# Softmax division, three PSUM reads and the loads of w_out moved between engines in a two-block network kernel

## The chip, the cores and the metric

The kernel runs on one core of a Trainium2 chip. The metric is the device time of one launch in microseconds: the median over runs, and beside it one profiled execution that gives the trace. All arithmetic is float32. The long projections run as three products of a high and a low part (written `hh`, `hl`, `wh`, `wl` below).

## The reference, cut to what matters

The program computes two blocks in series. The first (differential attention, pooling, a mixture of experts) is not touched by the change and takes the first 835 us of the trace. The second block has two layers, each on 512 tokens of width 1024. One layer is:

```
h    = rms_norm(x, norm_g[l]);  cols = split_columns(h @ w_in[l])
# gated delta rule ("Gdn"), chunks of 64 tokens, 6 heads, both directions
a_mat   = beta * (k k^T) * d_strict          # triangular system of a chunk
p_intra = (q k^T) * d_incl
u0, w   = triangular_solve(a_mat, [beta v, beta gam k])
scan over chunks: u = u0 - w s;  o = q_g s + p_intra u;  s = g_end s + k_d^T u
# latent attention ("mla"), 6 heads, blocks of 128 queries
p = softmax(q k^T);  y_mla = p v
# rwkv7 ("Rwkv"), a recurrence per token, evaluated in chunks with a triangular solve
# joined
mix = concat(y_gdn, y_mla, y_rwkv) * silu(cols.gate)
x   = x + mix @ w_out[l]
```

After two layers a last norm gives the output.

## The kernel before

**The stages of a layer.** In the trace, layer 0 of the second block is 835 to 1390 us and layer 1 is 1390 to 1930 us. A layer begins with `Project`: the columns of `h @ w_in`, 24 products of 128x128 by 128x512 for each column of 128 (`mm<-hh,wh`, `mm<-hl,wh`, `mm<-hh,wl`). Beside it runs `Gdn`. Its `take_v` transposes the v columns (`tr`) and copies both halves from PSUM into `VS`, one half by ScalarE (ACT), the other by VectorE (DVE). Its `keys` normalises `kt` on DVE and transposes it into `kq`. Its `squares` multiplies k by k (64x64 products into PSUM tile `x`, twelve for each of four token tiles) and multiplies the result into `M`. Its `decays` builds `DT` and multiplies it by the products of k and q, which DVE reads from PSUM. `inverse` solves the triangles on DVE, and `chain` goes through eight steps of the state.

When the projection is over, two streams share TensorE (PE). `Rwkv.prepare` builds the triangles of the third branch (`SC`, `RB`, `M`, and the products `mm<-XT,AO` and `mm<-LT,XT` of its solve). `mla` goes through 24 units of softmax: scores in PSUM, their maximum on DVE, the exponential with its sum on ACT, the reciprocal `rs` on DVE, `e*rs` on GpSimd (POOL, L2236), four transposes on PE, a copy on ACT, and the product `mo`. Then `Rwkv.states` (small products `kp`, `pu` and the state `ST`, eight steps) runs beside `Mix`, which multiplies the joined rows by w_out in groups of rows k = 0 to 2, 3 to 5 and 6 to 7.

**How w_out comes in.** `Mix.weights` loads one 128x1024 piece of w_out into a ring of two tiles `w`, ACT copies it rounded to the high part, and POOL subtracts to get the low part. `Mix.ahead` does the same early for k = 6 and 7 (for k = 7 the subtraction is left to DVE later). `Mix.rows` then makes, for each token tile, `tr<-mix`, `y` (DVE), `mh` (ACT), `ml` (POOL) and 18 products `mm<-w,mh`, `mm<-w,ml` of 128x512. In layer 0 the residual `xres` is also multiplied by `final_g` (tile `wf`) on DVE.

**What sets the order.** PE's order is written by hand-made streams: `Net.weave` runs the generator that is ready, and a generator yields the microseconds that it wants to wait. The clock of that game is `pe_us`, which `Net.matmul` and `Net.transpose` advance by a modelled price of each product. All other engines and the DMA queue of SyncE (SP) are ordered by a scheduler from data dependencies and priorities, and each engine then takes its instructions strictly in that order. So an instruction that waits holds all that stands behind it on its engine.

Of the kernel before, what the change touches and what calls it, by code (L numbers as in the profile page):

```python
# [1380 lines left out]
class Gdn:  # L1381
# [118 lines left out]
    def keys(self):  # L1500
# [11 lines left out]
        yield 14  # L1512
# [36 lines left out]
    def squares(self):  # L1549
# [3 lines left out]
        for t in range(NT):  # L1553
# [9 lines left out]
            for b in range(4):  # L1563
                q, o = quarter(b), 32 * (b % 2)
                nc.vector.tensor_tensor(M[q, :, us], KK[q, None, us, o:o + 32].to_broadcast([32, 2, 6, 32]), M[q, :, us], op=ALU.mult)  # L1565

# [180 lines left out]
class Rwkv:  # L1747
# [54 lines left out]
    def prepare(self, mud, xud):  # L1802
# [16 lines left out]
        with pool(tc, "rka", 1, "right") as tmp, pool(tc, "rks", 2, "right") as small, pool(tc, "rpa", 1, "right", PSUM) as psum:  # L1819
# [102 lines left out]
            def products(d):  # L1922
# [224 lines left out]
def mla(net, a, l, mchd, mixt, tabd):  # L2147

    tc, nc = net.tc, net.nc
    with ExitStack() as ctx:  # L2150
# [75 lines left out]
        def scores(n):  # L2226
# [9 lines left out]
            nc.gpsimd.tensor_scalar(e, e, rs, None, op0=ALU.mult)  # L2236
# [39 lines left out]

class Mix:


# [30 lines left out]
    def ahead(self):  # L2310

        w6 = self.p.tile([128, D], F32R, name="w6", tag="w6")
        self.weights(6, *self.wq[0], self.net.nc.gpsimd)
        self.weights(7, w6, None, None)
        self.wq = [self.wq[0], (w6, self.wq[1])]

    def load(self, k0, n, mix=None):

        net, nc = self.net, self.net.nc
        if k0 == 6:  # L2320
            self.wp = self.wq
            h, lo = self.wp[1]
            nc.vector.tensor_tensor(lo, self.w[:, 1], h.bitcast(F32), op=ALU.subtract)
        else:
            for j in range(n):
                self.weights(k0 + j, *self.wp[j], nc.gpsimd)
        if k0 == 0:
            for t in range(NT):
                nc.sync.dma_start(net.xres[:, t], self.xd[tok(t), :])
            if self.l == 0:  # L2330

                net.rsqrt(net.r1, net.r1)
                f = self.wf
                nc.sync.dma_start(f, dram(self.a["final_g"], 0, [[0, 128], [1, D]]))
                for t in range(NT):
                    nc.vector.scalar_tensor_tensor(net.xres[:, t], net.xres[:, t], net.r1[:, t:t + 1], f, op0=ALU.mult, op1=ALU.mult)
        nc.sync.dma_start(self.g[:, :n], self.gated[128 * k0:128 * (k0 + n), :].rearrange("(j p) s -> p j s", p=128))
# [56 lines left out]
def second(net, a, out, xstack, tabd, xd0, layers=2):  # L2394

    tc, nc = net.tc, net.nc
    with ExitStack() as ctx:
# [3 lines left out]
        for l in range(layers):  # L2401
# [132 lines left out]
```

## Time and profile before

| | |
|---|---|
| median of 3 runs | 1932.37 us (1925.56 to 1935.56) |
| profiled execution | 1931.57 us, span 1929.8 us |
| mean granted TensorE clock | 0.912 |
| PE busy | 1675.8 us, 87% of the span |
| DVE busy | 1062.8 us, 55% |
| ACT busy | 573.9 us, 30% |
| POOL busy | 548.8 us, 28% |

The span runs from the first to the last instruction, and the profiled execution's own time is 1.8 us longer. PE is the engine to follow: what is not PE work in the span is time in which PE waits, and a wait names the engine and line that ended it. The busy share of the other engines says little by itself, since they work in stretches.

### The profile page before, as it was taken

The page shows a single profiled execution, that of the slowest core. Times are in us where ns is not written, and L with a number is a line of the kernel's source. Part 1 is how long each engine was busy: PE and PEld are TensorE (multiplying, and loading weights), DVE is VectorE, ACT ScalarE, POOL GpSimd, SP SyncE. Part 2 cuts the span into 40 slices and gives each one's busy share as a digit, 9 for nine tenths or more (in the row PEclk, how much of TensorE's full clock was granted, in tenths as well). Part 3 has the DMA queues.
Part 4 walks back from the last instruction along what each step waited for, and adds up shares of the span by engine and source line. Part 5 has one row for each costly group of instructions (what it writes and reads, how often), then busy time and mean ns, then how long its engine had stood idle before and what let it go on. Part 6 is the DMA issues. An engine that isn't in the chain of part 4 may idle for free.

```text
span 1929.8 us, 34104 instructions
## 1 busy us (share of the span) xinstructions
PE 1675.8 (87%) x14010; PEld 1119.3 (58%) x14010; DVE 1062.8 (55%) x2260; ACT 573.9 (30%) x1134; POOL 548.8 (28%) x559
## 2 busy tenths in 40 slices
PE   5999998999999999968788978768896899888777
PEld 3986584454544444447576746545675677556455
DVE  2435534353434343357796476745867875667437
ACT  3345432212122121154322125331343231154312
POOL 1113111101010101045641154254354612544443
PEclk7899998999999999979898988888898899797888
DMA  9924626999999999532243120143422341301332
GB/s 308 243 94 151 245 66 250 392 393 394 407 402 397 395 406 398 211 112 77 55 148 73 57 75 2 43 138 99 120 74 70 106 110 63 80 1 28 106 118 80
DMA packets 243218, 337.10 MB, mean 175 GB/s; under 512 B 92768, under 2 KB 166160, under 8 KB 226224
## 3 DMA queue, kind: packets, MB, share of 16 engines
q1 hardware_dynamic: 241152, 329.88, 49.6%
q10 hardware_dynamic: 1152, 3.22, 0.5%
q8 instruction: 112, 1.84, 0.4%
q0 software_dynamic: 752, 1.76, 0.3%
q14 instruction: 50, 0.41, 0.1%
HBM read 310.84 MB, written 23.99 MB: 174 GB/s over the span
## 4 chain that ended last, share of the span: by engine, by line
PE 26%; DVE 16%; issue 5%; DMA 4%; POOL 3%; ACT 2%; SPq 0%; DVEq 0%; POOLq 0%; ACTq 0%
PE mm L149 18%; DVE au L1344 2%; PE mm L159 2%; DVE stmp L1342 2%; PE x L149 2%; PE tr L149 1%; PE pu L149 1%; PE kp L149 1%; DVE M L1565 1%; POOL w L2308 1%; DMA w<-in_w_out_dram 1%; DVE wl L1214 1%; PE tr L159 1%; DVE y L1289 1%; PE mo L149 1%
## 5 line engine op out<-in xcount | busy, mean ns | idle before, releaser
L149 PE MATMUL gu<-w,XT 128*64 128x512 f32 x1024 | 225.8, 594 | 0.0
L149 PE MATMUL mm<-hh,wh 128*128 128x512 f32 (+1 forms) x464 | 202.1, 436 | 1.9 <-DVE rw L1319 1.9
L149 PE MATMUL mm<-hl,wh 128*128 128x512 f32 (+1 forms) x464 | 187.3, 404 | 0.0
L149 PE MATMUL mm<-hh,wl 128*128 128x512 f32 (+1 forms) x464 | 187.2, 403 | 0.0
L928 POOL TENSOR_TENSOR yl<-y,yh 128x512 fp32r<-128x512 f32 x30 | 38.1, 1271 | 451.3 <-ACT yh L927 451.3
L149 PEld LDWEIGHTS gu<-w,XT 128*64 128x64 f32 x1024 | 72.1, 137 | 142.7 <-issue 135.6
L938 DVE TENSOR_TENSOR xres<-mm,xres 128x512 f32<-128x512 f32 x128 | 79.2, 681 | 90.6 <-PE mm L149 90.6
L1212 ACT ACTIVATE wh<-w 128x1024 fp32r<-128x1024 f32 (+1 forms) x54 | 57.0, 1055 | 192.8 <-PE mm L149 134.1
L149 PE MATMUL mm<-w,hT 128*64 128x512 f32 x512 | 113.4, 595 | 0.7 <-ACT hT L912 0.7
L149 PEld LDWEIGHTS mm<-hh,wh 128*128 128x128 f32 (+1 forms) x464 | 91.3, 197 | 27.9 <-issue 5.7
L149 PEld LDWEIGHTS mm<-hh,wl 128*128 128x128 f32 (+1 forms) x464 | 90.6, 195 | 21.0
L2236 POOL TENSOR_SCALAR e<-e,rs 128x512 f32<-128x512 f32 x48 | 79.1, 1651 | 80.0 <-DVE rs L2235 58.1
L149 PEld LDWEIGHTS mm<-hl,wh 128*128 128x128 f32 (+1 forms) x464 | 91.6, 197 | 17.5 <-DVE hl L1160 0.2
L1214 POOL TENSOR_TENSOR wl<-w,wh 128x1024 fp32r<-128x1024 f32 (+1 forms) x28 | 68.1, 2431 | 112.3 <-ACT wh L1212 101.7
L149 PE MATMUL mm<-wh,hh 128*128 128x256 f32 x320 | 94.0, 294 | 2.2 <-ACT hh L357 2.2
L149 PE MATMUL mm<-wh,hl 128*128 128x256 f32 x320 | 91.2, 285 | 4.2 <-DVE hl L359 4.0
L149 PE MATMUL mm<-w,mh 128*128 128x512 f32 x256 | 88.6, 429 | 6.7 <-ACT mh L2359 4.1
L149 PE MATMUL mm<-wl,hh 128*128 128x256 f32 x320 | 90.7, 284 | 1.6 <-DVE wl L381 1.6
L149 PEld LDWEIGHTS mm<-w,hT 128*64 128x64 f32 x512 | 35.3, 137 | 66.7 <-issue 61.7
L1342 DVE TENSOR_TENSOR stmp<-au 96x60 f32<-96x60 f32 (+29 forms) x120 | 60.2, 501 | 16.0 <-DMA au<-rmud 8.7
L872 ACT ACTIVATE X<-mm,ws 128x512 f32<-128x512 f32 x32 | 22.0, 689 | 151.9 <-DVE ws L869 128.7
L926 DVE SCALAR_TENSOR_TENSOR y<-mm,ws,g2b 128x512 f32<-128x512 f32 x32 | 24.0, 751 | 78.2 <-PE mm L149 78.2
(580 smaller groups left out, 3678.4 us busy)
## 6 DMA issues: line engine op xcount, KB each, us to landing
w<-in_w_gate_dram SPq DMA_DIRECT2D x64, 1024.0 KB, 13.0
w<-in_w_up_dram SPq DMA_DIRECT2D x64, 1024.0 KB, 13.0
w<-in_w_down_dram SPq DMA_DIRECT2D x64, 1024.0 KB, 9.8
w<-in_w_in_dram SPq DMA_DIRECT2D x52, 512.0 KB, 4.1
w<-in_w_ada_dram SPq DMA_DIRECT2D x24, 1024.0 KB, 8.4
w<-in_w_out_dram SPq DMA_DIRECT2D x16, 512.0 KB, 4.1
w<-in_w_in_dram SPq DMA_DIRECT2D x6, 1024.0 KB, 11.9
w<-in_w_out_dram SPq DMA_DIRECT2D x4, 1024.0 KB, 6.3
```

Source lines behind the costliest of these rows:

```text
L149: return self.nc.tensor.matmul(out, a, b, **kw)
L159: return self.nc.tensor.transpose(out, a, ident)
L872: nc.scalar.activation(X[:, 512 * i:512 * i + 512], ps, AF.Copy, scale=ws[:, 1:2])
L926: nc.vector.scalar_tensor_tensor(y, py, ws[:, 0:1], net.g2b[:, hs], op0=ALU.mult, op1=ALU.mult)
L928: (nc.vector if last else nc.gpsimd).tensor_tensor(yl[:, hs], y, yh[:, hs].bitcast(F32), op=ALU.subtract)
L938: nc.vector.tensor_tensor(net.xres[:, t, hs], po, net.xres[:, t, hs], op=ALU.add)
L1212: nc.scalar.activation(h[:, :, :m], w[:, :, :m], AF.Copy)
L1214: eng.tensor_tensor(lo[:, :, :m], w[:, :, :m], h[:, :, :m].bitcast(F32), op=ALU.subtract)
L1289: nc.vector.scalar_tensor_tensor(y[:, lo:hi], ps[:, lo + d:hi + d], cw[:, j, m:m + 1], y[:, lo:hi], op0=ALU.mult, op1=ALU.add)
L1342: nc.vector.tensor_tensor(tv, au[:n, :, j + 1:, j:j + 1].to_broadcast(sh), au[:n, :, j:j + 1, 0:j].to_broadcast(sh), op=ALU.mult)
L1344: nc.vector.tensor_tensor(au[:n, :, j + 1:, 0:j], au[:n, :, j + 1:, 0:j], tv, op=ALU.add)
L2236: nc.gpsimd.tensor_scalar(e, e, rs, None, op0=ALU.mult)
```

## The change

Eight edits, all in the second block but the first:

1. In the model of PE's order, a float32 product of at most 64x64x64 counts a third of what it did.
2. `take_v`: both halves are copied by ACT.
3. `keys` yields 19 in place of 14 before its transposes.
4. `squares`: the multiplications into `M` are done for two token tiles at once (16 in place of 32 over both layers, twice as wide).
5. `decays`: ACT copies k.q from PSUM into an SBUF tile, and one DVE multiplication does both directions (8 in place of 16).
6. `prepare`: the multiplications into `SC` and `RB` do both halves at once (16 in place of 32 of each).
7. `mla`: `e*rs` is an ACT activation with a scale in place of a POOL multiplication (48 of them).
8. w_out: a class `Raw` owns a ring of four tiles `w` and asks for the first four pieces as soon as `prepare` has been written; `Mix.load` asks for `mix` and `gate` first; the subtraction for the second piece of a group is on DVE; `xres` is raised in halves inside `rows`.

The core of the diff:

```diff
         if a.dtype == F32:
-            self.pe_us += 2 * max(n / 1200, m / 1200, 0.027)
+            us = 2 * max(n / 1200, m / 1200, 0.027)
+            self.pe_us += us / 3 if m <= 64 and n <= 64 and a.shape[0] <= 64 else us
...
-                (nc.vector.tensor_copy if h else nc.scalar.copy)(dst, pv[half(h)])
+                nc.scalar.copy(dst, pv[half(h)])
...
-        yield 14
+        yield 19
...
-            for b in range(4):
-                q, o = quarter(b), 32 * (b % 2)
-                nc.vector.tensor_tensor(M[q, :, us], KK[q, None, us, o:o + 32].to_broadcast([32, 2, 6, 32]), M[q, :, us], op=ALU.mult)
+            if t % 2:
+                us = slice(6 * t - 6, 6 * t + 6)
+                for b in range(4):
+                    q, o = quarter(b), 32 * (b % 2)
+                    nc.vector.tensor_tensor(M[q, :, us], KK[q, None, us, o:o + 32].to_broadcast([32, 2, 12, 32]), M[q, :, us], op=ALU.mult)
...
-            for d in range(2):
-                dv = DT[:, d, us].rearrange("p (a h) c -> p a h c", a=2)
-                nc.vector.tensor_tensor(dv, dv, ps[:, :, :192].rearrange("p a (h c) -> p a h c", h=3), op=ALU.mult)
+            kr = tmp.tile([128, 6, 64], F32, name="rh")
+            nc.scalar.activation(kr.rearrange("p (a h) c -> p a (h c)", a=2), ps[:, :, :192], AF.Copy)
+            nc.vector.tensor_tensor(DT[:, :, us], DT[:, :, us], kr[:, None].to_broadcast([128, 2, 6, 64]), op=ALU.mult)
...
-                    for par in range(2):
-                        nc.vector.tensor_tensor(SC[:, par], pv[:, par, :, 64:], mk[:, None, :].to_broadcast([128, 2, 128]), op=ALU.mult)
+                    nc.vector.tensor_tensor(SC, pv[:, :, :, 64:], mk[:, None, None, :].to_broadcast([128, 2, 2, 128]), op=ALU.mult)
...
-            nc.gpsimd.tensor_scalar(e, e, rs, None, op0=ALU.mult)
+            nc.scalar.activation(e, e, AF.Copy, scale=rs)
...
+class Raw(dict):
+    def __init__(self, net, ctx, a, l):
+        super().__init__()
+        self.net, self.a, self.l = net, a, l
+        self.pool = ctx.enter_context(pool(net.tc, "wo", 4, "right"))
+        for k in range(4):
+            self.load(k)
+    def load(self, k):
+        w = self[k] = self.pool.tile([128, D], F32, name="w")
+        self.net.nc.sync.dma_start(w, dram(self.a["w_out_2"], (self.l * D + 128 * k) * D, [[D, 128], [1, D]]))
...
-        w = self.w[:, k % 2]
-        nc.sync.dma_start(w, dram(self.a["w_out_2"], (self.l * D + 128 * k) * D, [[D, 128], [1, D]]))
+        nc, w = self.net.nc, self.raw.pop(k)
...
+        if k0 < 6:
             for j in range(n):
-                self.weights(k0 + j, *self.wp[j], nc.gpsimd)
+                self.weights(k0 + j, *self.wp[j], nc.vector if j == 1 else nc.gpsimd)
...
+        for k in range(k0 + 4, min(k0 + 7, KC)):
+            self.raw.load(k)
...
+                if fresh:
+                    nc.vector.scalar_tensor_tensor(xres[:, t, hs], xres[:, t, hs], net.r1[:, t:t + 1], self.wf[:, hs], op0=ALU.mult, op1=ALU.mult)
...
+                while raw is None:
+                    yield 0.5
...
             net.weave(prepare, others, until=prepare)
+            raw = Raw(net, third.ctx, a, l)
             net.weave(states, others, until=states)
```

Three places show what this does to the order of instructions (no times here, only the order in which each engine takes them).

SP's queue in layer 0 at the end of `mla`, where `mixt<-mo` writes a tile of attention output and `xres` is the residual, in the kernel before:

```order
388 L2329 DMA xres<-xd 128x1024 x2
389 L2258 DMA mixt_7547<-mo 384x1x128
390 L2329 DMA xres<-xd 128x1024 x2
391 L2305 DMA w<-in_w_out_dram 128x1024 x2
392 L2334 DMA wf<-in_final_g_dram 128x1024
393 L2337 DMA gate<-gated_7548 128x3x512
394 L2343 DMA mix<-mixd_7546 128x4x384
395 L2305 DMA w<-in_w_out_dram 128x1024 x3
```

The same place in the changed kernel:

```order
388 L2347 DMA xres<-xd 128x1024 x2
389 L2260 DMA mixt_7547<-mo 384x1x128
390 L2347 DMA xres<-xd 128x1024 x2
391 L2340 DMA mix<-mixd_7546 128x4x384
392 L2341 DMA gate<-gated_7548 128x3x512
393 L2350 DMA wf<-in_final_g_dram 128x1024
394 L2291 DMA w<-in_w_out_dram 128x1024 x8
395 L2354 DMA mix<-mixt_7547 128x1536
```

The first pieces of w_out stood behind the last `mixt` and two `xres`; now `mix`, `gate` and `wf` stand ahead of them as well, and all eight pieces stand in one block.

ACT in layer 0, from the last unit of `mla` to the first rows of `Mix`, where `w_...<-w` is the rounded copy of a piece of w_out and `mh<-y` the high part of a mixed row; the kernel before:

```order
541 L2306 ACTIVATE w_11873<-w 128x1024
542 L2306 ACTIVATE w_11874<-w 128x1024
543 L2306 ACTIVATE w_11875<-w 128x1024
544 L2359 ACTIVATE mh<-y 128x384 x5
545 L2306 ACTIVATE w_11873<-w 128x1024
```

The changed kernel:

```order
568 L2319 ACTIVATE w_11823<-w 128x1024
569 L2319 ACTIVATE w_11824<-w 128x1024
570 L2319 ACTIVATE w_11825<-w 128x1024
571 L2319 ACTIVATE w_11829<-w 128x1024
572 L2319 ACTIVATE w_12272<-w 128x1024
573 L2374 ACTIVATE mh<-y 128x384 x5
```

Two copies, those of pieces k = 6 (`w_11829`) and k = 7 (`w_12272`), have come in between the copies of k = 0 to 2 and the first `mh`. The tile of piece 6 is the one that held piece 2, and piece 7 is loaded into the tile that held piece 6, each after POOL's subtraction of the piece before.

PE in layer 0 at the end of `mla`, where `mm<-cst,e` are transposes of a softmax tile, in the kernel before:

```order
3063 L149 MATMUL mo<-t_11577,vt 64x128
3064 L149 MATMUL mm<-LT,XT 32x32 x64
3065 L149 MATMUL kp<-ST,KR 64x64 x8
3066 L159 MATMUL mm<-cst,e 128x128 x8
3067 L149 MATMUL pu<-rhs,LT 64x64 x8
3068 L149 MATMUL mo<-t_11593,vt 64x128
```

The changed kernel, from the last two `mo` of `mla` on:

```order
3079 L151 MATMUL mo<-t_11605,vt 64x128
3080 L151 MATMUL mo<-t_11620,vt 64x128
3081 L151 MATMUL mm<-XT,AO 32x32 x64
3082 L151 MATMUL mm<-LT,XT 32x32 x64
3083 L151 MATMUL kp<-ST,KR 64x64 x8
3084 L151 MATMUL pu<-rhs,LT 64x64 x8
```

`mm<-LT,XT`, with `mm<-XT,AO` ahead of it, and the first steps of `states` stood between the last units of `mla` and now follow after the last `mo`. In layer 1 all three places look alike, without `wf`.

## Rows read from the trace of the kernel before

**Rows 1.** Stretches of layer 0, busy by engine, clock, DMA share, GB/s.

```profile
core 0: us, PE busy (x) PEld busy (x) DVE busy (x) ACT busy (x) POOL busy (x), PEclk, DMA share, GB/s
870.00:1126.00 256.00, 217.46 (x2302) 171.52 (x2301) 179.03 (x300) 67.27 (x108) 100.99 (x114) 0.90 0.32 84
952.00:1009.00 57.00, 50.46 (x293) 39.72 (x292) 54.91 (x83) 12.94 (x18) 30.31 (x31) 0.94 0.34 103
1126.00:1272.00 146.00, 116.55 (x1228) 73.93 (x1228) 101.56 (x231) 62.41 (x139) 65.61 (x54) 0.86 0.13 32
1272.00:1311.00 39.00, 20.25 (x533) 15.78 (x529) 15.73 (x23) 8.23 (x13) 17.87 (x20) 0.67 0.53 174
```

**Rows 2.** Waits of PE, layer 0: waited for, us in total, times, longest.

```profile
PE tr L159 <- DVE VS L1444: 12.0, 3, 7.0
PE mm L149 <- DVE SC L1945: 10.8, 3, 5.8
...
PE mm L159 <- DVE sq L1874: 7.8, 3, 5.3
PE x L149 <- DVE DT L1601: 6.2, 1, 6.2
PE tr L159 <- DVE kt L1515: 5.0, 1, 5.0
...
PE mm L159 <- POOL e L2236: 3.0, 2, 1.6
```

**Rows 3.** Waits of PE, layer 1.

```profile
PE tr L159 <- DVE VS L1444: 11.4, 3, 6.3
PE tr L159 <- DMA mix<-mixd: 8.6, 1, 8.6
PE x L149 <- DVE DT L1601: 6.8, 1, 6.8
```

**Rows 4.** Groups by line, 870 to 1126: busy, mean ns, idle before.

```profile
L1444 DVE COPY VS<-tr 64x512 f32<-64x512 f32 x6 | 4.2, 695 | 5.4 <-ACT VS L1444 5.4
L1601 DVE TENSOR_TENSOR DT<-DT,x 128x384 f32<-128x384 f32 x8 | 4.0, 545 | 0.0
```

**Rows 5.** ACT's nearest operation to the new one, 870 to 1126.

```profile
L1292 ACT ACTIVATE th<-y 128x512 f32<-128x512 f32 x9 | 5.7, 629 | 7.6 <-DVE y L1289 7.6
```

**Rows 6.** Groups by line, 1126 to 1272, POOL and DVE.

```profile
L2236 POOL TENSOR_SCALAR e<-e,rs 128x512 f32<-128x512 f32 x22 | 36.4, 1657 | 41.5 <-DVE rs L2235 27.4 <-PE mm L149 10.6 <-DVE au L1344 2.4
L1874 DVE TENSOR_TENSOR s<-BB,cl 128x512 f32<-128x512 f32 x4 | 4.7, 1186 | 0.0
L1869 DVE TENSOR_TENSOR KR<-ci,rw 128x512 f32<-128x512 f32 x4 | 2.7, 680 | 0.0
```

**Rows 7.** PE in time around the start of Mix, layer 0.

```profile
1271.87 1.29 PE L149 MATMUL mm<-XT,AO 32*32 32x32 f32 x128
1286.38 1.09 PE L149 MATMUL mo<-t,vt 128*64 128x128 f32 x14 [0.38 <-ACT t L2244]
1303.57 0.90 PE L159 MATMUL tr<-cst,mix 128*128 128x128 f32 x3 [9.15 <-DMA mix<-mixd]
1311.00 0.80 PE L149 MATMUL mm<-w,ml 128*128 128x512 f32 x1 [1.73 <-POOL ml L2360]
```

**Rows 8.** ACT and POOL in time, the same place.

```profile
1296.26 1.06 ACT L2306 ACTIVATE w<-w 128x1024 fp32r<-128x1024 f32 x1 [9.93 <-DMA w<-in_w_out_dram]
1297.40 5.62 POOL L2308 TENSOR_TENSOR w<-w,w 128x1024 fp32r<-128x1024 f32 x2 [5.76 <-DMA w<-in_w_out_dram]
```

**Rows 9.** DMA issues of w_out: pieces, KB each, median us to landing.

```profile
w<-in_w_out_dram SPq DMA_DIRECT2D x16, 512.0 KB, 4.1
```

**Rows 10.** PE in time around the start of Mix, layer 1.

```profile
1806.96 1.61 PE L149 MATMUL mm<-XT,AO 32*32 32x32 f32 x128
1823.71 1.09 PE L149 MATMUL mo<-t,vt 128*64 128x128 f32 x14 [0.39 <-ACT t L2244]
1845.26 0.80 PE L149 MATMUL mm<-w,ml 128*128 128x512 f32 x1 [1.76 <-POOL ml L2360]
```

More of the change, by code (lines that the diff above doesn't have):

```diff
@@ L1943, in products @@
                     SC = small.tile([128, 2, 2, 128], F32, name="SC")
-                    for par in range(2):
-                        nc.vector.tensor_tensor(SC[:, par], pv[:, par, :, 64:], mk[:, None, :].to_broadcast([128, 2, 128]), op=ALU.mult)
-                    for par in range(2):
-                        nc.vector.tensor_tensor(RB[:, d, us].rearrange("p (a c) k -> p a c k", a=2)[:, par], pv[:, par, :, 0:64],
-                                                m2[:, None, :].to_broadcast([128, 2, 64]), op=ALU.mult)
+                    nc.vector.tensor_tensor(SC, pv[:, :, :, 64:], mk[:, None, None, :].to_broadcast([128, 2, 2, 128]), op=ALU.mult)
+                    nc.vector.tensor_tensor(RB[:, d, us].rearrange("p (a c) k -> p a c k", a=2), pv[:, :, :, 0:64],
+                                            m2[:, None, None, :].to_broadcast([128, 2, 2, 64]), op=ALU.mult)
                     SU = SC.rearrange("p a c k -> p (a c) k")
@@ L2274, in mla, with __init__ @@
                 yield 0
+class Raw(dict):
[8 more added lines that the diff above has]
+        self.net.nc.sync.dma_start(w, dram(self.a["w_out_2"], (self.l * D + 128 * k) * D, [[D, 128], [1, D]]))
 class Mix:
-    def __init__(self, net, a, l, mixd, mixt, gated, xd, xstack):
+    def __init__(self, net, a, l, mixd, mixt, gated, xd, xstack, raw):
         tc, nc = net.tc, net.nc
-        self.net, self.a, self.l, self.mixd, self.mixt, self.gated = net, a, l, mixd, mixt, gated
+        self.net, self.a, self.l, self.mixd, self.mixt, self.gated, self.raw = net, a, l, mixd, mixt, gated, raw
         net.xres = xstack.enter_context(pool(tc, "xres")).tile([128, NT, D], F32, name="xres")
@@ L2287, in __init__ @@
         self.psum = self.ctx.enter_context(pool(tc, "mxp", 1, "left", PSUM))
+        self.m = p.tile([128, NT * 384], F32, name="mix")
         self.g = p.tile([128, 3, S], F32, name="gate")
-        self.m = p.tile([128, NT * 384], F32, name="mix")
         self.y = p.tile([128, 2, 3, 128], F32, name="y")
@@ L2294, in __init__ @@
         self.wf = p.tile([128, D], F32, name="wf", tag="w6")
-        split = [p.tile([128, D], F32R, name=f"w{j}") for j in range(3)]
-        self.w = p.tile([128, 2, D], F32, name="w")
-        split += [p.tile([128, D], F32R, name=f"w{j}") for j in (3, 4, 5, 7, 8)]
+        split = [p.tile([128, D], F32R, name=f"w{j}") for j in (0, 1, 2, 3, 4, 5, 7, 8)]
         self.wp = [(split[j], split[j + 3]) for j in range(3)]
@@ L2322, in load @@
             h, lo = self.wp[1]
-            nc.vector.tensor_tensor(lo, self.w[:, 1], h.bitcast(F32), op=ALU.subtract)
-        else:
+            nc.vector.tensor_tensor(lo, self.w7, h.bitcast(F32), op=ALU.subtract)
+        if k0 == 0:
+            mix = self.m.rearrange("p (t c) -> p t c", t=NT)
+            nc.sync.dma_start(mix, self.mixd.rearrange("(t p) c -> p t c", p=128))
+        nc.sync.dma_start(self.g[:, :n], self.gated[128 * k0:128 * (k0 + n), :].rearrange("(j p) s -> p j s", p=128))
+        if k0 < 6:
             for j in range(n):
-                self.weights(k0 + j, *self.wp[j], nc.gpsimd)
+                self.weights(k0 + j, *self.wp[j], nc.vector if j == 1 else nc.gpsimd)
         if k0 == 0:
@@ L2332, in load @@
                 net.rsqrt(net.r1, net.r1)
[L2333 to L2337, printed above, removed]
+                nc.sync.dma_start(self.wf, dram(self.a["final_g"], 0, [[0, 128], [1, D]]))
+            self.raised = self.l == 0
         if k0 == 3:
@@ L2452, in second @@
                 gs.close()
+            raw = None
             def others():
@@ L2456, in others @@
                 yield from mla(net, a, l, mchd, mixt, tabd)
-                mix = Mix(net, a, l, mixd, mixt, gated, xd, xstack)
+                while raw is None:
+                    yield 0.5
+                mix = Mix(net, a, l, mixd, mixt, gated, xd, xstack, raw)
                 for k in (0, 3):
```

6 lines of the change are left out of this document (2 added, 4 removed).

## The prediction

> **What bounds the kernel now.** I read the page first, which has PE busy for 87% of the span and the second block running from 835 us to the end, then the stretches of a layer, then what PE waits for, and last the start of the mixing in time. The change touches only the second block, so only the waits of its two layers can move, and PE's own work stays: no product is added or taken away. The reader should see three things. While the projection hides `Gdn`, PE works 217.46 of 256.00 us, and in the solve DVE works 54.91 of 57.00 us [rows 1]: there DVE sets the pace. The 38.5 us that PE loses in that stretch are mostly waits for DVE: 12.0 for the `VS` copies, 6.2 for `DT`, 5.0 for `kt` [rows 2], and in layer 1 11.4 and 6.8 [rows 3]. In the softmax stretch PE works 116.55 of 146.00 us, ACT only 62.41 [rows 1]; the waits are for DVE (10.8 for `SC`, 7.8 for `sq`) and little for POOL, 3.0 [rows 2]. At the start of the mixing PE stands 9.15 us for the DMA of `mix` in layer 0 [rows 7] and 8.6 in layer 1 [rows 3], and the whole stretch has PE at 20.25 of 39.00 us and a granted clock of 0.67 [rows 1].
>
> **Part A, projection and Gdn (edits 1 to 5), per layer.** Six DVE copies of 695 ns go, 4.2 us [rows 4]; ACT does twelve copies where it did six, and ACT is idle for most of this stretch (67.27 of 256.00 us busy [rows 1]). The gain is not all of the 12.0 us of waits: DVE itself already waited 5.4 us for ACT's half of the copy [rows 4], so the two halves now stand one behind the other on ACT. I give half back, 6 us. In `decays` eight DVE multiplications of 545 ns [rows 4] become four wider ones that read SBUF: nothing to 2.2 us saved, and ACT's four reads stand ahead of them; of the 6.2 us behind `DT` I count 2. The 5.0 us behind `kt` go because the transposes come later in PE's order, with more projection columns ahead of them: up to 5, I count 4. Against these: the transposes of `kt` and the first products of `squares` are now later, so the chain that ends in the solve starts later, and DVE is full there; one step of `Gdn`'s chain comes after the columns are used up, and such a step shows as a wait of a few microseconds. I take 2 us for it. So 6 + 2 + 4 - 2 = 10 us less per layer. Both ends: 0, if DVE's full stretch simply moves, and 20, if all three waits but 3 us go.
>
> **Part B, prepare and softmax (edits 6, 7), per layer.** 24 POOL multiplications of 1657 ns [rows 6] become 24 ACT instructions. The trace has no ACT copy with a scale from a column; the nearest row is an activation of the same shape from SBUF, 629 ns [rows 5], so ACT gets 24 x 0.629 = 15.1 us and would be at 77.5 of 146 us, not the bound. A unit's latency falls by 1.03 us, and POOL's 3.0 us of waits [rows 2] go. The wait for `SC`, 10.8 us in layer 0, is a DVE queue whose instructions become half as many. But ACT is in order, and the division now stands between two exponentials and waits for the DVE reciprocal there, so other ACT results come later. I take 3 us less per layer, with ends of 4 more (ACT's queue holds the transposes' copies) and 10 less.
>
> At DVE the rows show something that bears on this: a multiplication of 128x512 with both inputs in SBUF takes 680 ns on line 1869 and 1186 ns on line 1874 [rows 6]. The Trainium skill (SBUF — State Buffer, section "SBUF: two separate sides") says that DVE with two SBUF inputs and a GpSimd operation that reads SBUF lock each other out of one port pair for a whole instruction. If that is what the 506 ns are, POOL's 36.4 us leave DVE freer, worth some 4 x 0.5 = 2 us more in the wait for `sq`. The same rule speaks against edit 8: the subtraction put on DVE would queue against POOL's two, each about 2.8 us, and part C would lose up to 2.8 us a layer more. The sum goes without either.
>
> **Part C, the start of the mixing (edits 1, 8).** By its words the change loads w_out early. By the order it doesn't: the eight loads stand on SP behind the last `mixt`, two `xres`, `mix` and `gate` (in layer 0 `wf`), so none can start before the last `mo` has ended.
> - Before, layer 0: the last `mo` ends at 1286.38 + 1.09 = 1287.47, and the steady products start at 1311.00 [rows 7], 23.5 us later.
> - Bytes: piece 0 is in ACT at 1296.26 [rows 8], 8.8 us after the `mo`, behind 1.77 MB (`mixt` 0.2, two `xres` 1.05, itself 0.52); `mix` is there at 1303.57 [rows 7], 16.1 us after, behind 4.4 MB. That is 2.6 MB in 7.3 us, 0.36 MB a microsecond.
> - After: piece 0 has 3.87 MB up to it, so it lands at 8.8 + 2.1/0.36 = 14.6 us; piece 2, 1.05 MB on, at 17.5. ACT copies 1.06 us each, POOL's pair of subtractions takes 5.62 us [rows 8] from 15.7 on, so it ends at 21.3. Only then is the tile free for piece 6: load 4.1 us [rows 9] to 25.4, ACT's copy to 26.5, one subtraction of 2.8 to 29.3, piece 7 to 33.4, copy to 34.5. All of this stands on ACT ahead of the first `mh`, so `y`, which DVE has ready long before, waits. With 0.5 for `mh` and 1 for `ml` the steady products start 36.0 us after the `mo`: 12.5 us later than before. Behind the waiting ACT instruction stand all `mh`, behind the waiting product on PE the rest of `states`, which nobody else fills.
> - Layer 1: before, 1845.26 - (1823.71 + 1.09) = 20.5 us [rows 10]; after, without `wf` (0.52/0.36 = 1.4), 34.6, so 14.1 later.
> - Given back: the products of the solve and two steps of `states` leave the tail of `mla` and run inside that wait. From `mm<-XT,AO` to the end of the last `mo` are 15.6 us in layer 0 [rows 7] and 17.8 in layer 1 [rows 10]. What stays of it is three groups of `mo` at 1.09, twelve transposes (2.0) and about 2.5 of one unit's latency, 7.8 in all. So the last `mo` comes 7.8 and 10.0 us earlier.
> - Net: 12.5 - 7.8 = 4.7 later, and 14.1 - 10.0 = 4.1 later.
>
> **Part D, the rest of the mixing.** No load is waited for later, as pieces 6 and 7 are there; a fourth output group of `states` comes ahead of the rows of k = 3, and DVE has a 128x1024 subtraction more. I take 1 us more per layer, between -2 and +4.
>
> **Sum.** 2 x (-10) + 2 x (-3) + 8.8 + 2 x 1 = -15.2 us. The profiled execution took 1931.57 us, 1.8 over its span and 0.8 under the median; 1931.6 - 15.2 = 1916.4, and against the median 1917.2. I predict 1917 us.
>
> **Rivals.**
> - *The mixing eats it all (slower).* The last `mo` is bound by the latency of its unit, not by PE: near the end PE already waits for ACT ([rows 7], 0.38 us), and with ACT doing three things per unit instead of two, nothing is given back. Then C costs 12.5 + 14.1 = 26.6 instead of 8.8, and with A and B at half (-13) and D +2 the sum is +15.6: 1947 us. It decides from the point where A and B together give less than some 28 us. For it: the stretch with PE at 20.25 of 39.00 us is latency already [rows 1]. Against it: the products taken out of the tail are PE's own work there.
> - *Waits change names (no change).* In A the wait behind DVE becomes one behind ACT's second copy and the solve starts later by what the wait lost; A gives 3 per layer, B 0: -6 + 8.8 + 2 = +4.8, 1937 us. For it: DVE is at 54.91 of 57.00 us in the solve [rows 1].
> - *The early loads do early (faster by more).* If the pieces land before the end of `mla` in spite of SP's order, or piece 6 and 7 don't hold ACT, C is -8 us a layer from the 9.15 and 8.6 us waits that are then covered: -26 - 16 + 2 = -40, 1892 us. Against it stands SP's order in both layers.
> - *DVE is freed by the port* (the rule above; in the rows, line 1874 falling to 680 ns): B gives 5 instead of 3 a layer, 1913 us, inside the forecast's range; of its 0.48 I give this 0.1.
>
> **How the numbers follow.** What a measurement of this kernel can tell from no change is about 0.5%, 9.7 us: faster is below 1922.7, slower above 1942. Forecast with its own range of 1906 to 1930 (A from -7 to -14 a layer): 0.48, of which 0.38 is faster and 0.10 within. Slower rival 0.22, of which 0.18 slower and 0.04 within. Names change 0.18: 0.11 within, 0.04 slower, 0.03 faster. Early loads or a larger A 0.12, all faster. So 0.53, 0.25, 0.22. The range reaches from the early loads' side, 1892, to just under the slower rival's 1947, 1946: about 2 in 10 lie outside.
>
> **What would show it.** In the profile after: `tr<-kt` and `tr<-cst` of the v columns no longer wait for DVE (A); DVE busy in the first third of each layer 4 to 6 us less; PE in that stretch losing 28 rather than 38.5 us. ACT's group of `e<-e,rs` near 629 ns (B). At the mixing, SP's first `w` after the last `mixt`, ACT idle behind the DMA of w_out between the copies of k = 2, 6 and 7, and PE waiting some 20 us on `mm<-w,mh` for ACT's `mh` (C). The prediction is wrong if that wait is absent or if PE's waits in the first third are as large as before.

## The result and the profile after

The changed kernel takes 1957.85 us (median, 1953.98 to 1958.73) against 1933.63 before in the same comparison: a ratio of 1.0135, 95% interval 1.0112 to 1.0158. The forecast was 1917 us with a range to 1946. Time, range and sign are wrong. This ratio and those below are taken over undisturbed runs and can differ a little from the quotient of the two medians.

The profiled execution has a span of 1957.0 us, 27.2 more than before. The starts and ends of PE's work cut each layer into five stages: from the first `mm<-hh,wh` to the first `mm<-kT,qT` (A), from there to the end of the last `mm<-kT,qT` (F), to the end of the last `mo` (T), to the first `mm<-w,ml` (S), and the rest of the layer (R). In microseconds, layer 0 / layer 1:

| stage | before | after | difference | forecast |
|---|---|---|---|---|
| A projection and Gdn | 326.1 / 318.8 | 320.2 / 317.8 | -5.9 / -1.0 | -10 / -10 |
| F first to last scores | 97.0 / 92.3 | 106.2 / 106.4 | +9.2 / +14.1 | -3 / -3 |
| T last scores to last `mo` | 15.5 / 17.8 | 6.3 / 6.3 | -9.2 / -11.5 | -7.8 / -10 |
| S last `mo` to steady mixing | 23.5 / 20.5 | 41.4 / 34.7 | +17.9 / +14.2 | +12.5 / +14.1 |
| R rest | 85.0 / 76.9 | 84.5 / 74.3 | -0.5 / -2.6 | +1 / +1 |

With 2.4 us at the start of the second block (848.8 us before, 851.2 after; the other kernels below start it between 846.6 and 851.2), that is 27.1 us. T and layer 1's S came close to the forecast, layer 0's S was 5.4 us over it, and F did the opposite. Of the 42.3 us between the forecast of -15.2 and the measured +27.1, F is 29.3 and A 13.1; the rest nearly cancels.

**S.** SP after the last `mo` of layer 0 (start, length, line, operation, count; `...` marks rows left out here and below), and when it asks for pieces 5 and 6 of w_out (a narrower view of the same eight):

```profile
1284.57 0.52 SPq L2260 DMA_DIRECT2D mixt<-mo  x1
1285.14 2.13 SPq L2347 DMA_DIRECT2D xres<-xd  x2
...
1288.97 30.46 SPq L2291 DMA_DIRECT2D w<-in_w_out_dram  x8
```

```profile
1310.66 0.80 SPq L2291 DMA_DIRECT2D w<-in_w_out_dram  x2
```

ACT there, the five copies of w_out and the first `mh`:

```profile
1301.02 1.06 ACT L2319 ACTIVATE w<-w 128x1024 fp32r<-128x1024 f32 x1 [9.81 <-DMA w<-in_w_out_dram]
1302.29 2.15 ACT L2319 ACTIVATE w<-w 128x1024 fp32r<-128x1024 f32 x2 [0.21 <-DMA w<-in_w_out_dram]
1315.58 1.06 ACT L2319 ACTIVATE w<-w 128x1024 fp32r<-128x1024 f32 x1 [11.14 <-DMA w<-in_w_out_dram]
1322.71 1.06 ACT L2319 ACTIVATE w<-w 128x1024 fp32r<-128x1024 f32 x1 [6.08 <-DMA w<-in_w_out_dram]
1323.68 0.92 ACT L2374 ACTIVATE mh<-y 128x384 fp32r<-128x384 f32 x2
```

DVE there, the raises of `xres` (its multiplication by `final_g`, edit 8), a step of `states`, the subtraction of piece 1; then POOL's subtractions of pieces 0 and 2:

```profile
1299.60 9.57 DVE L2387 SCALAR_TENSOR_TENSOR xres<-xres,r,wf 128x512 f32<-128x512 f32 x8 [8.55 <-DMA wf<-in_final_g_dram]
1309.09 0.41 DVE L2052 TENSOR_SCALAR AKV<-pu 128x256 f32<-128x256 f32 x1
1309.42 1.21 DVE L2321 TENSOR_TENSOR w<-w,w 128x1024 fp32r<-128x1024 f32 x1
```

```profile
1302.15 5.14 POOL L2321 TENSOR_TENSOR w<-w,w 128x1024 fp32r<-128x1024 f32 x2 [37.50 <-ACT w L2319]
```

PE there, from the last `mo` to the steady products (before: [rows 7]):

```profile
1282.86 1.09 PE L151 MATMUL mo<-t,vt 128*64 128x128 f32 x14 [0.33 <-ACT t L2246]
1283.88 1.29 PE L151 MATMUL mm<-XT,AO 32*32 32x32 f32 x128
...
1309.56 0.49 PE L151 MATMUL kp<-AKV,BK 64*64 64x64 f32 x8 [16.97 <-DVE AKV L2052]
...
1317.83 0.90 PE L161 MATMUL tr<-cst,mix 128*128 128x128 f32 x3
...
1324.24 1.22 PE L151 MATMUL mm<-w,mh 128*128 128x512 f32 x2 [2.30 <-ACT mh L2374]
1325.32 0.80 PE L151 MATMUL mm<-w,ml 128*128 128x512 f32 x1
```

The forecast's chain is all there: piece 0 at 1301.02 is 17.1 us after the `mo` (forecast 14.6), the copies of pieces 6 and 7 stand ahead of `mh`. But it isn't alone. `AKV` of `states` waits behind eight raises, PE waits 16.97 us for it, and from there three steps of `states` and the start of a fourth take until 1321.94. Both chains end within 2.3 us of each other. The raises also reach into the chain of the loads: DVE's subtraction of piece 1 stands behind them, and only when it has ended (1310.63) does SP ask for piece 5 and, behind it in its queue, for piece 6, although POOL was done with the tile of piece 6 at 1307.29. In layer 1, without raises, another instruction holds `states`, DVE's subtraction, which waits for piece 1 ahead of `ST`:

```profile
1839.18 1.09 PE L151 MATMUL mo<-t,vt 128*64 128x128 f32 x14 [0.33 <-ACT t L2246]
...
1859.07 0.71 PE L151 MATMUL kp<-ST,KR 64*64 64x64 f32 x16 [8.51 <-DVE ST L2068]
...
1873.88 1.22 PE L151 MATMUL mm<-w,mh 128*128 128x512 f32 x2 [2.43 <-ACT mh L2374]
1874.96 0.79 PE L151 MATMUL mm<-w,ml 128*128 128x512 f32 x1
```

**F.** The stretch of the scores, columns as in [rows 1]; both layers before, then both after:

```profile
1174.97:1271.94 96.97, 75.63 (x893) 53.08 (x897) 66.84 (x173) 43.06 (x102) 45.32 (x31) 0.91 0.12 30
1714.71:1807.03 92.32, 81.22 (x893) 56.54 (x896) 66.09 (x173) 42.88 (x100) 45.40 (x31) 0.85 0.13 31
```

```profile
1171.40:1277.64 106.24, 83.87 (x888) 57.75 (x890) 66.27 (x159) 55.39 (x123) 12.63 (x16) 0.82 0.12 29
1727.58:1833.96 106.38, 86.75 (x888) 59.50 (x890) 66.36 (x159) 56.11 (x123) 12.62 (x16) 0.81 0.12 29
```

The two layers grew in different ways. In layer 0 PE is idle for 22.4 us in place of 21.3, and needs 8 us more for the same products: the granted clock is 0.82 in place of 0.91. In layer 1 it needs 5.5 us more for them, and its idle time grew from 11.1 to 19.6 us. PE's waits after, layer 0, from 1171 to 1345 us, the largest but `AKV`; then the wait for `SC` in layer 1, before and after:

```profile
PE mm L151 <- DVE SC L1948: 12.8, 4, 5.4
PE x L151 <- DVE M L1908: 5.2, 1, 5.2
PE pu L151 <- DVE rhs L2044: 3.3, 3, 2.2
PE mm L161 <- ACT e L2236: 3.1, 1, 3.1
```

```profile
PE mm L149 <- DVE SC L1945: 2.9, 1, 2.9
```

```profile
PE mm L151 <- DVE SC L1948: 10.3, 4, 5.2
```

The wait for `SC` was 10.8 us before in layer 0 [rows 2], so there it is a little longer, and in layer 1 it is 7.4 us longer, though its DVE instructions are half as many. One of these waits in time shows what comes with it:

```profile
1245.31 1.59 PE L151 MATMUL x<-KR,BB 64*64 64x64 f32 x32
1246.83 0.66 PE L161 MATMUL mm<-cst,e 128*128 128x128 f32 x4
1247.32 1.02 PE L151 MATMUL mm<-kT,qT 96*128 96x512 f32 x2
1248.18 0.60 PE L161 MATMUL mm<-cst,e 128*128 128x128 f32 x4
1254.23 1.97 PE L151 MATMUL mm<-vt,SC 64*64 64x64 f32 x32 [5.45 <-DVE SC L1948]
1256.13 2.07 PE L151 MATMUL mm<-kT,qT 96*128 96x512 f32 x2
1258.14 1.81 PE L151 MATMUL mo<-t,vt 128*64 128x128 f32 x16
```

PE has 1.9 us of softmax work between the end of `x` and the product with the `SC` that is made of it, where it had 2.5 before: the `mo` that stood there now follows behind. PE waits 5.45 us, and the products after it run at the lower level, 1.2 GHz (`mm<-kT,qT` 2.07 us in place of 1.02). What it waits for is a place in DVE's queue; DVE there after, and the same instructions before:

```profile
1247.99 0.70 DVE L2004 STREAM_TRANSPOSE LT<-XT 32x512 f32<-32x512 f32 x1 [2.42 <-DMA XT<-rxud]
...
1252.74 0.71 DVE L2006 STREAM_TRANSPOSE XT<-LT 32x512 f32<-32x512 f32 x1
1253.48 0.69 DVE L1948 TENSOR_TENSOR SC<-x,mk 128x512 f32<-128x512 f32 x1
```

```profile
1245.32 0.75 DVE L1945 TENSOR_TENSOR SC<-x,mk 128x256 f32<-128x256 f32 x2
...
1253.16 0.70 DVE L2002 STREAM_TRANSPOSE LT<-XT 32x512 f32<-32x512 f32 x1 [2.22 <-DMA XT<-rxud]
```

`x` is done at 1246.90, but the transposes of the solve stand ahead of the last `SC` on DVE and themselves wait for a load. Before, the last `SC` stood ahead of them. In layer 1 the same order costs a wait of 5.22 us. The other two long waits for `SC` in layer 0 (3.04 and 3.76 us) stand behind other DVE work of the solve, as the two before did (4.21 and 5.82 us).

### The profile page after: what moved, and what is told of

It is laid out like the page before. It is cut to its first block, busy times and chain, and to the rows that moved or that the text cites. A ratio compares the mean times of both kernels' runs of the same rounds, so it can differ in the third digit from the quotient of the medians.

```text
span 1957.0 us, 33945 instructions
## 1 busy us (share of the span) xinstructions
PE 1683.5 (86%) x14010; PEld 1127.2 (58%) x14010; DVE 1053.3 (54%) x2200; ACT 612.4 (31%) x1202; POOL 469.4 (24%) x507
## 4 chain that ended last, share of the span: by engine, by line
PE 23%; DVE 20%; DMA 6%; ACT 3%; issue 3%; POOL 2%; SPq 1%; DVEq 0%; POOLq 0%; ACTq 0%
PE mm L151 15%; DVE stmp L1344 3%; DVE au L1346 3%; DMA w<-in_w_out_dram 2%; PE tr L151 2%; PE mm L161 1%; PE x L151 1%; PE kp L151 1%; PE pu L151 1%; DVE wl L1216 1%; DVE M L1569 1%; PE mo L151 1%; DMA au<-mud 1%; DMA gate<-gated 1%; DVE y L1291 1%
## 5 line engine op out<-in xcount | busy, mean ns | idle before, releaser
L1344 DVE TENSOR_TENSOR stmp<-au 96x60 f32<-96x60 f32 (+29 forms) x120 | 65.4, 545 | 30.4 <-DMA au<-mud 21.5
L151 PEld LDWEIGHTS mm<-w,hT 128*64 128x64 f32 x512 | 35.3, 137 | 66.6 <-issue 61.7
L151 PEld LDWEIGHTS mm<-wh,hl 128*128 128x128 f32 x320 | 61.4, 192 | 5.7 <-DVE hl L361 5.3
## 6 DMA issues: line engine op xcount, KB each, us to landing
w<-in_w_gate_dram SPq DMA_DIRECT2D x64, 1024.0 KB, 13.5
w<-in_w_up_dram SPq DMA_DIRECT2D x64, 1024.0 KB, 13.3
```

The costliest lines, as they stand in the source:

```text
L1344: nc.vector.tensor_tensor(tv, au[:n, :, j + 1:, j:j + 1].to_broadcast(sh), au[:n, :, j:j + 1, 0:j].to_broadcast(sh), op=ALU.mult)
```

## The experiments

Ratios are to the kernel before, run on the same chip. Stages as above, layer 0 / layer 1, from one profile each. "New price" is edit 1, "tied" a kernel in which each raise of `xres` waits for its row of the mixing (e7).

| run | median us | ratio (95%) | F | T | S |
|---|---|---|---|---|---|
| before | | | 97.0 / 92.3 | 15.5 / 17.8 | 23.5 / 20.5 |
| after | 1957.9 | 1.0135 (1.0112-1.0158) | 106.2 / 106.4 | 6.3 / 6.3 | 41.4 / 34.7 |
| e1 old price | 1926.6 | 0.9995 (0.9972-1.0018) | 90.7 / 102.6 | 14.9 / 13.4 | 16.8 / 13.4 |
| e2 without edit 8 | 1939.1 | 1.0063 (1.0040-1.0087) | 106.0 / 106.5 | 6.3 / 6.3 | 35.3 / 26.1 |
| e3 edit 8 alone | 1930.5 | 1.0024 (1.0004-1.0043) | 100.3 / 95.4 | 16.2 / 15.2 | 16.3 / 13.5 |
| e4 edit 7 alone | 1937.6 | 1.0064 (1.0035-1.0094) | 100.1 / 96.0 | 15.4 / 16.8 | 24.0 / 20.3 |
| e5 edit 1 alone | 1943.9 | 1.0069 (1.0047-1.0090) | 101.4 / 106.0 | 6.1 / 6.1 | 34.0 / 27.2 |
| e6 edits 2-5 alone | 1938.3 | 1.0030 (1.0008-1.0051) | 98.2 / 99.2 | 16.8 / 16.7 | 22.6 / 20.6 |
| e7 edit 8, tied | 1929.0 | 1.0008 (0.9991-1.0025) | 100.9 / 101.9 | 13.8 / 13.3 | 14.4 / 14.4 |
| e8 edits 2-6, 8 tied | 1918.4 | 0.9940 (0.9923-0.9958) | 93.3 / 98.1 | 13.7 / 12.8 | 14.1 / 13.6 |
| e9 after, ring of 3 | 1949.0 | 1.0120 (1.0090-1.0150) | 107.4 / 104.2 | 6.3 / 6.3 | 37.4 / 30.4 |
| e10 e9, tied | 1943.8 | 1.0102 (1.0079-1.0125) | 104.2 / 106.6 | 6.3 / 6.3 | 33.0 / 29.4 |
| e11 edit 6 alone | 1937.7 | 1.0057 (1.0039-1.0074) | 98.7 / 99.6 | 14.6 / 16.3 | 23.7 / 20.5 |
| e12 edits 6, 8 tied | 1925.9 | 1.0003 (0.9987-1.0020) | 99.8 / 102.9 | 13.3 / 16.0 | 14.3 / 14.1 |
| e13 new price in A | 1929.0 | 1.0027 (1.0007-1.0046) | 95.7 / 99.3 | 13.8 / 16.3 | 23.5 / 20.8 |
| e14 all, price in A, tied | 1920.9 | 0.9976 (0.9958-0.9994) | 102.4 / 102.5 | 14.0 / 12.8 | 14.6 / 13.0 |
| e15 e8 again | 1916.8 | 0.9956 (0.9935-0.9977) | 93.6 / 98.2 | 14.8 / 12.8 | 13.9 / 14.3 |
| e16 e8, price in A | 1921.0 | 0.9975 (0.9952-0.9998) | 100.7 / 102.8 | 15.6 / 15.4 | 14.1 / 13.1 |
| e17 e10, GpSimd | 1942.8 | 1.0082 (1.0059-1.0105) | 107.4 / 109.7 | 6.3 / 6.3 | 30.7 / 29.2 |

### Which edit: e1 to e5

**e1** is the changed kernel with this line back, **e5** the kernel before with the new one (and the joined rows waiting for the end of `prepare`, without which their tiles have no room):

```diff
-            self.pe_us += us / 3 if m <= 64 and n <= 64 and a.shape[0] <= 64 else us
+            self.pe_us += us
```

> All edits but the first: the model of the order prices 64x64 products as before. Theory 'order': the changed model alone puts the end of prepare behind the last mo and with it the loads of w_out; priced as before, SP has four pieces of w_out ahead of the last mixt and both layers start the mixing some 9 and 6 us earlier after the last mo than the kernel before instead of 17.9 and 14.2 later, so 1957.9 - 32 - 15 = about 1911 us, 1903 to 1920. Theory 'engines': the division on ScalarE and the later keys cost the time, the mixing only shows it; then what the mixing wins is lost before it and the time stays over 1930.

> The kernel before with the first edit alone (64x64 products count a third), with the joined rows waiting for the end of prepare, without which their tiles have no room. 'Order' (this edit alone moves prepare behind the softmax): softmax stretch of 106 us from the first scores to the last in both layers in place of 97 and 92, mixing 12 and 6 us later after the last mo, tail shorter by 9 and 11: 1928 + 15 to 20, so 1940 to 1950 us. 'Engines' (the other edits cost it): within 6 us of the kernel before.

e1 is 27 us faster than the changed kernel by the ratios (0.0140 of 1930). Its SP has the first four pieces before the last `mixt`, 17 us ahead:

```profile
1259.89 9.27 SPq L2289 DMA_DIRECT2D w<-in_w_out_dram  x4
...
1277.10 0.52 SPq L2258 DMA_DIRECT2D mixt<-mo  x1
```

and S is 16.8 / 13.4. So the same eighth edit is early or late by the first edit alone. It didn't get to 1911, and lies between what the two theories gave: its layer 0 lost 9 us in R (93.6 us). e5 is slower by 0.7%, 1943.9 us where 1940 to 1950 was expected. F is as expected in layer 1 and half of it in layer 0; S is as expected in both, in layer 0 because `rhs` of `states` waits 13.4 us behind the raises.

**e2** takes edit 8 out of the changed kernel (the joined rows still wait for the end of `prepare`), **e3** puts it alone into the kernel before, **e4** edit 7 alone (all by the diff of the change).

> All edits but the eighth: w_out comes in as in the kernel before; the joined rows still wait for the end of prepare. 'Order': the copies of pieces 6 and 7 and the raise in halves no longer stand ahead of the first mixed rows, so the steady products start 21 to 24 us after the last mo as before: 1957.9 - 32 = about 1926 us, 1919 to 1933. 'Engines': 1940 or more.

> The kernel before with the eighth edit alone. 'Order': the loads are early here, since the model is the old one: 1933.6 - 9 - 6 = about 1919 us, 1912 to 1926. 'Engines', or a price of the edit itself (subtraction on VectorE, raise in halves, copies of pieces 6 and 7 on ScalarE): 1933 or more.

> The kernel before with the seventh edit alone (softmax division on ScalarE). 'Order': little, between -6 and +4 us, since ACT is idle for more than half of that stretch. 'Engines': slower by 8 us or more, ACT's queue holding the exponentials.

e2 is 0.7% under the changed kernel, but not back at the 1926 us of the first theory: F stays at 106 and S at 35.3 / 26.1. Those are edit 1's, as e5 has much the same. e3's S is 7 us shorter in both layers, and nothing comes of it: F is 3 us longer in both, and R of layer 0 is 94.1. PE's waits there, from the last `mo` to 1345 us, name the cause:

```profile
PE pu L149 <- DVE rhs L2042: 9.4, 3, 4.8
```

The eight raises are now what DVE does when `states` needs it. e4 refutes the prediction's -3 us for the division: 0.6% slower alone, as the second theory had it.

### What the late start waits for: e7, e9, e10, e17

**e7** ties each raise to its row (edit 8 alone otherwise):

```diff
+            if fresh:
+                late = self.y[:, t % 2, 0, 0:1]
+                nc.scalar.activation(late, net.r1[:, t:t + 1], AF.Copy)
...
-                    nc.vector.scalar_tensor_tensor(xres[:, t, hs], xres[:, t, hs], net.r1[:, t:t + 1], self.wf[:, hs], op0=ALU.mult, op1=ALU.mult)
+                    nc.vector.scalar_tensor_tensor(xres[:, t, hs], xres[:, t, hs], late, self.wf[:, hs], op0=ALU.mult, op1=ALU.mult)
```

> The kernel before with the eighth edit alone, but each raise of xres takes its scale from a column that ScalarE writes after the row's ml, so that no raise can stand on VectorE ahead of the first mixed rows. If the eight raises in one block are what gives the early loads back in layer 0 (4.8 us of wait at pu<-rhs and the low clock behind it): 6 to 10 us under the eighth edit alone (1930.5), 1920 to 1924. If not: 1927 to 1933.

R of layer 0 went back to 86.5, as expected if the raises gave the early loads back; the time did not follow (1.0008 against e3's 1.0024, the intervals overlap).

**e9** has `pool(net.tc, "wo", 3, "right")`, three first loads, and `range(k0 + 3, min(k0 + 6, KC))`; **e10** adds the tie, **e17** also `nc.gpsimd` for all three subtractions.

> The changed kernel with a ring of three tiles for w_out in place of four, so that the copies of pieces 6 and 7 on ScalarE come after the first five mh and nothing else moves. If these copies hold the first mixed rows: in layer 1 the steady products start some 23 us after the last mo in place of 34.7, in layer 0 only 2 us earlier, because there the states behind the raises are late as well: 1957 - 14 = about 1944 us. If the copies hide behind the states in both layers: 1952 or more.

> The same, and each raise of xres tied behind the ml of its row, so that the states of layer 0 don't wait 17 us for VectorE. If copies and raises together are the late start: both layers at 23 to 26 us after the last mo, 1957 - 12 - 16 = about 1929 us, 1924 to 1936. If something else holds it (bytes of w_out, GpSimd): over 1940.

> The ring of three, tied raises, and all three subtractions on GpSimd as in the kernel before. If VectorE's subtraction holds the states until the late piece 1 has landed: PE's 9.6 us wait at pu<-rhs goes, but GpSimd has its first subtraction ahead of the second scaling of ST, so 3 to 8 us of it come back there: mixing 25 to 30 us after the last mo, 1943.8 - 6 to 14, 1930 to 1938. If it hid behind something else anyway: 1941 to 1947.

With the copies of pieces 6 and 7 gone from ahead of `mh`, S falls by 4 us in each layer (expected 2 and 12): in layer 1 PE still waits 7.70 us for `ST`, behind DVE's subtraction. In e9, layer 1, DVE, and then POOL:

```profile
1851.26 2.23 DVE L2321 TENSOR_TENSOR w<-w,w 128x1024 fp32r<-128x1024 f32 x1 [7.11 <-ACT w L2319]
```

```profile
1850.04 2.36 POOL L2321 TENSOR_TENSOR w<-w,w 128x1024 fp32r<-128x1024 f32 x1 [32.80 <-ACT w L2319]
1852.81 2.93 POOL L2321 TENSOR_TENSOR w<-w,w 128x1024 fp32r<-128x1024 f32 x1 [0.41 <-ACT w L2319]
```

e10 takes the raises away as well: another 4.4 us in layer 0, and again a wait behind the subtraction, 9.62 us. Its time is 15 us over the 1929 expected. e17 takes that wait away, and in layer 0 5.66 us come back for `ST` behind POOL's subtraction and 2.92 behind a tied raise on DVE. The ratios of e9, e10 and e17 have overlapping intervals. Each in-order queue has something in it that waits for a late load; taking one out shows the next. In all 10.7 and 5.5 us of S came back this way. With early loads (e1) S is 24.6 and 21.3 us shorter; 8.6 and 7.1 of that are work which e1 leaves in T.

### Edits that each cost and together gain: e6, e8, e11 to e16

e6, e11 and e12 are edits of the diff alone; e8 is edits 2 to 6 and 8 with the tie, e15 the same again. e13, e14 and e16 use the new price only while projection and Gdn are ordered:

```diff
+            net.third = True
             net.weave(first, project, until=first)
             net.weave(second, project, until=second)
             net.weave(project)
+            net.third = False
```

> The kernel before with edits 2 to 5 alone (v and k.q by ScalarE, later keys, M two tiles at once), in the old model. If the waits for VS, DT and kt are worth what the prediction took: -20 us, 1908. If the chain of the solve starts later by what the waits lose: -5 to +5 us, 1923 to 1933.

> The kernel before with edit 6 alone (SC and RB in one instruction for both halves). The last but one group had edits 2 to 5 at +0.3% and edits 2 to 6 with w_out at -0.6%, so either this edit is worth some 10 us (waits for SC shorter, granted clock of the softmax stretch higher): 1915 to 1922. Or the two only fit together, and alone it is worth what VectorE saves, 1 to 3 us: 1924 to 1930.

> Old model, edit 6 and the eighth with the raise tied, without edits 1 to 5 and 7. If edits 2 to 5 cost 0.3% wherever they stand, this is faster than with them (1918): 1909 to 1916. If they pay once the rest of the order suits them: 1918 to 1928.

> Old model, edits 2 to 6 and the eighth with the raise tied; no first and no seventh edit. If the parts add: 1928 - 7 (early loads) and what edits 2 to 6 give (0 to -20): 1903 to 1921 us, the fastest so far. If edits 2 to 6 cost something: over 1921.

> Old price, edits 2 to 6 and the eighth with the raise tied, a second time on another chip's runs: 0.994 of the kernel before if that was no accident (0.992 to 0.996), 1915 to 1919 us; above 0.998 if it was.

> The kernel before, with 64x64 products counted a third only while the projection and Gdn are ordered. If the first edit gains in that stage and loses after it: 5 to 8 us under the kernel before, 1919 to 1923. If its gain there is an accident of single profiles: 1924 to 1931.

> The same with the new price in the first stage: if the gains add, 5 to 8 us under it, 1908 to 1913, the fastest; if not, the same within 3 us.

> All eight edits, the new price only in the first stage and the raise of xres tied. If what made the changed kernel slow is the new price in prepare, states and the mixing: 1957.9 - 40, 1912 to 1922. If the division on ScalarE costs what it cost alone (0.6%): 1922 to 1932.

e14 is the changed kernel with two things different, the price after stage A and the tie: from 1.0135 to 0.9976, 31 us, 1920.9 us where 1912 to 1922 was expected. The price is what did most of it, since the tie was worth about 5 us or less where it was timed (e9 to e10, e3 to e7). The gain that the new price shows in A of layer 0 (315.6 / 322.4 in e13) is none in the time: 1.0027, and e16 isn't under e8 and e15.

Edits 2 to 5, 6 and 7 are each 0.3 to 0.6% slower alone, though each takes work from DVE or POOL; e6 (1938.3) and e11 (1937.7) are slower than either case of their expectations. With early loads and the tie, edits 2 to 6 make the fastest kernel here (e8 and e15, 0.994 and 0.996). Why each alone costs is not settled. In the kernels whose F is ordered by the old price, F spreads from 90.7 to 102.9 us with clocks from 0.92 to 0.78. The one program profiled twice, e8 and e15, has F within 0.3 us (93.3 / 98.1, 93.6 / 98.2), so the spread looks like one of orders rather than of executions; which wait in it makes the difference was not tested.

## Why the prediction was wrong

- **What failed: "Given back", the 17.8 us in part C.** The products did leave the tail, and T shrank by 9.2 / 11.5, a little more than forecast. But the tail was priced by itself. The same edit that moved them also spaced `prepare` and softmax anew over the whole stretch ahead: F grew by 9.2 / 14.1. F and T together are 112.5 / 112.7 us, 112.5 / 110.1 before: nothing was given back. The prediction works out PE's order only at its end and DVE's order in this stretch not at all; there the last `SC` had gone behind the transposes of the solve. e2 and e5 show the longer F without edit 8 and without all others (106.0 / 106.5, 101.4 / 106.0). The 12 profiled stretches F that the new price ordered (after, e2, e5, e9, e10, e17) have a mean of 106.0 us, the 26 of the old price 98.5, so some 7.5 us a layer go with the price; the kernel before has a short F in layer 1 (92.3, and 102.6 in e1 with all edits but the price). The transposes stand first in 11 of the 12 and in one of the 26 (e7, layer 1).
- **Part B, -3 a layer: wrong sign.** The prediction took the waits for POOL off and counted on half as many DVE instructions for `SC`, and added ACT as free time. But the 8 wide instructions take 5.5 us of DVE where the 16 took 6.1, and the wait for `SC` comes from what stands ahead of it on DVE. A wait of PE costs its length and then the slow products after it; that second price wasn't in the sum. e4 has the division at 0.6% by itself.
- **Part A, -10 a layer.** Measured -5.9 / -1.0. What remains at PE is the wait for ACT's copies (7.8 us) and for ACT's read of k.q (7.7 us in layer 0, 5.5 in layer 1): 4 of the 12 us of `VS` came back (forecast 6), of `DT` nothing in layer 0. The 5.0 us behind `kt` went (forecast 4). In layer 1 PE waits 6.8 us for ACT's `wh`, which it didn't before. And edits 2 to 5 alone give nothing in A (323.4 / 325.6 in e6).
- **Part C, +26.6 at the start of the mixing: right in place, 32.1 measured.** Loads late by SP's order: right. Layer 1 came out at 34.7 for 34.6, by the forecast's own steps (piece 0 at 13.8 us for 13.2, piece 7 at 32.1 for 32.0). But the mechanism was one of three in parallel. The wait of some 20 us on `mm<-w,mh` that was to show it is 2.30 and 2.43 us: PE stands earlier, for `AKV` behind DVE's raises and for `ST` behind DVE's subtraction, and the prediction has no term for either. Of layer 0's 5.4 us more, 2.5 are piece 0's; most of the rest came with piece 6, 31.6 us after the `mo` for 25.4, held 3.8 us by the raises through SP's queue.
- **Part D**, 1 us each: -0.5 / -2.6, nothing.
- **The slower rival** (0.22) had the right sign and was nearest, 1947 us against 1957.9, partly by luck. Its condition held (A and B together under 28 us), but it let them still gain 13 us where A and F lost 16.4; and it had the tail keep its length for ACT's latency, where T shrank and F took the gain.
- **The port rival.** Line 1874's operation (1878 after) has a mean of 914 ns for `s` in place of 1186, and `sq` of 946, 944 before. The means hide two cases. Before, then after (least / median / most ns):

```profile
L1874 DVE TENSOR_TENSOR s<-BB,cl x8: 676/1162/1759, 1138.6 to 1739.0; 128x512 f32<-128x512 f32 x8
```

```profile
L1878 DVE TENSOR_TENSOR s<-BB,cl x8: 671/677/1632, 1135.4 to 1753.1; 128x512 f32<-128x512 f32 x8
```

One of each case before, with POOL beside them:

```profile
1198.86 0.68 DVE L1874 TENSOR_TENSOR sq<-BB,cl 128x512 f32<-128x512 f32 x1
1199.46 1.76 DVE L1874 TENSOR_TENSOR s<-BB,cl 128x512 f32<-128x512 f32 x1
```

```profile
1196.49 2.60 POOL L2236 TENSOR_SCALAR e<-e,rs 128x512 f32<-128x512 f32 x1
1199.06 1.61 POOL L1972 TENSOR_TENSOR bs<-bs,rw 128x512 f32<-128x512 f32 x1
```

In both kernels all 32 operations of this line take 671 to 692 ns or 1632 to 1759. Each of the ten long ones starts under a POOL multiplication of two tensors and ends 0.5 us after it; the four that start in the last 0.4 us of a division take 677 to 679. So the 506 ns are waiting for POOL, but not for the division that edit 7 took away, and the rival's 2 us had the wrong POOL instruction. The subtraction shows the same: alone it takes DVE 1.21 us; in e9 it starts under POOL's, takes 2.23 and ends 1.09 us after POOL's end at 1852.40, and POOL's next one begins under it and takes 2.93 in place of 2.36. That agrees with the Trainium skill (SBUF — State Buffer, "SBUF: two separate sides"), by which whichever comes first keeps the shared port for its whole instruction. The division doesn't fit it: at 1221.93 a DVE multiplication (`stmp`) that starts with 1.49 us of a division's recorded span to go takes 0.79 us where it takes 0.33 alone, so it was held for less than half a microsecond.

## What to carry to other kernels

When a table of prices sets an order, read the new order over the whole stretch that it governs, not only where the change is meant to act: here a truer price of small products (32 of 64x64x64 take 1.59 us in the rows above; the old price makes it 3.4, the new 1.1) took 1.4%, because three streams' ends and the moment of an early load hung on it. A load is early only if the queue has it early, and an engine that takes its instructions in order passes a late load on to everything behind it; count all such queues, since removing one shows the next. And a wait can cost more than its length, as the products behind it ran at the lower clock here.

## What the hardware showed unexpectedly

The division on ACT takes 721 ns, not the 629 of the activation of the same shape that the prediction took it from [rows 5].

```profile
L2238 ACT ACTIVATE e<-e,rs 128x512 f32<-128x512 f32 x48 | 34.6, 721 | 15.0 <-DVE rs L2237 15.0
```

The median from issue to landing of a piece of w_out is 6.9 us, 4.1 before [rows 9], and the median hides two groups: in each layer the first four pieces, asked for behind `xres`, `mix` and `gate`, take 9 to 13 us, the later four 3.5 to 4.4.

```profile
DMA to landing us min/median/max: 3.5/6.9/12.8
```

The same products of F (888 to 893 PE records) kept PE busy for 75.6 us at a granted clock of 0.91 to 0.92 and for 86.8 us at 0.79 (e2).
